# The norms of a two-layer diffusion trunk: where the squares are summed, where the root is read, and who splits the result

## The chip, the cores and the metric

The kernel runs on one core of a Trainium2 chip. The metric is the device time of one launch in microseconds (us). The engines are TensorE (PE; its weight loads are PEld), VectorE (DVE), ScalarE (ACT), GpSimd (POOL) and SyncE (SP), which issues the transfers. Each engine works through its own queue in order; SBUF is the on-chip memory, PSUM the banks that PE writes its products to.

## The reference, cut to what matters

A latent stream x of 512 tokens and a context of 256 tokens, 1024 features each, go through two layers. Every layer has a token-mixing sub-layer (attention, gated DeltaNet and gated linear attention that share one input projection and one output projection) and a convolutional feed-forward (FFN). Around both stands the same sandwich of norms:

```python
def rmsnorm(x, g):
    xf = x.astype(F32)
    y = xf * lax.rsqrt(jnp.mean(xf * xf, axis=-1, keepdims=True) + NORM_EPS)
    return y.astype(x.dtype) * g

def modulate(h, shift, scale):
    return h * (1 + scale) + shift
```

A sub-layer computes x + gate * rmsnorm(sub(modulate(rmsnorm(x, g_pre), shift, scale)), g_post); shift, scale and gate come from a product of the conditioning vector with w_ada. The mean of squares goes over the 1024 features of a token.

## The kernel before, in words

Activations lie feature-major: eight tiles (k = 0 to 7) of 128 features, each with all 768 tokens (the context in columns 0 to 255, named CS, the latents in 256 to 767, named XS). A norm over the features is therefore a sum over the eight tiles and over the 128 partitions of each. There are sixteen such norms: eight prenorms (three of 512 tokens, five of 256; the two at the very start are computed ahead of their scaling) and eight posts (two of 512, six of 256). The first layer works on 512 latents and then on 256 context tokens; the second layer's output projection and last FFN part work on two halves of 256 latents, since the context is no longer needed.

`rms` (L492) does this: ACT squares the eight tiles (L505), the even ones and the odd ones are added into two accumulators, the even ones by DVE, the odd ones by POOL (L507). PE multiplies each 128 tokens of both accumulators with a column of ones (tile `ones`), which gives a sum for each token on its partition; ACT takes the root, DVE the reciprocal (`rsqrt`, L243 and L244). A second set of PE products spreads the reciprocal over all partitions, into a second bank of PSUM, and ACT copies it to SBUF as `rb` (L523).

`post` (L526) scales the sub-layer's output with gate and rb (DVE, L533, tile `y`) and adds it to x (L534), even tiles on DVE, odd ones on POOL. `prenorm` (L536) makes the modulated input in two float32r parts, `hh` and `hl`. Even tiles: DVE makes v (L545), ACT adds the shift and rounds to hh (L546), DVE subtracts for hl (L547). Odd tiles: DVE makes v (L549), ACT makes hh (L550) and the unrounded value (L551), POOL subtracts (L552).

All large products are three float32r passes (high times low, low times high, high times high; tile `bb`), L212 by way of the helper `mm`. Their weights arrive as `wr` and are split too: ACT rounds (`wh`, L191), DVE subtracts (`wl`, L192). So DVE's queue holds the norms' steps and the weights' low parts that PE needs next. At the start `ada` (L467) multiplies the conditioning vector with sixteen loads of w_ada (tile `aw`, eight products of two loads each, then a small product of `part`); all eight must be done before the first prenorm can scale. Single banks of PSUM are handed out in turn (`ab`, tags a to d).

The order on every engine is set by a scheduler that lays the whole program out beforehand with its own estimates; the order in which the code issues the steps and the number of buffers of each tag steer it, so that a change in the norms moves instructions elsewhere too.

Of the kernel before, what the change touches and what calls it, by code (L numbers as in the profile page):

```python
# [11 lines left out]
F32 = mybir.dt.float32  # L12
# [8 lines left out]
KT = 8  # L21
# [11 lines left out]
# columns of the feature-major parameter array  # L33
# [3 lines left out]
PA = (0, 2, 4, 6)  # L37
WP = ()
SQB = 3
# [15 lines left out]
SQ0, MG, PR = 0, 0, 0  # L55
ACB, RBB = 4, 2
WB, RB = 3, 2
R3, B3 = 0, 0
NF = 3                  # tiles of the GDN preparation under way at a time
# columns of the constant array  # L60
# [50 lines left out]
def rope_tables():  # L111
    """cos and signed sin on the rope rows, ones on the others: even heads, odd heads"""
# [23 lines left out]
class Net:  # L136
# [46 lines left out]
    def ab(self, tags=None):  # L183
        """a bank of PSUM, out of those of the phase or of the chain of work named"""
        tags = tags or self.tags
        self.turn[tags] = n = self.turn.get(tags, -1) + 1
        t = tags[n % len(tags)]
        return self.ps.tile([128, 512], F32, name=self.nm(t), tag=t, bufs=1)
# [8 lines left out]
    def wsplit(self, src, n=1024):  # L197
        """loads [128, n] weights and splits them in two float32r parts, 512 columns a piece"""
# [18 lines left out]
    def fprod(self, ps, wh, wl, xh, xl, segs, nk, order=None, off=256):  # L217
        """ps[:, 256 + token] = sum over k of w[:, k]^T x[k], in three float32r passes"""
# [13 lines left out]
    def pace(self, n):  # L232
        """some steps of the products that fill the tensor engine beside chains of small ones"""
# [7 lines left out]
    def rsqrt(self, out, ss, scale, bias):  # L241
        """out = 1 / sqrt(scale * ss + bias), small tiles"""
# [18 lines left out]
    def main(self):  # L261
# [20 lines left out]
        # the first two modulations lead; the norm needs all of x, then them  # L282
# [28 lines left out]
    def layer(self, l, later):  # L311
# [9 lines left out]
        # token mixing  # L321
# [22 lines left out]
        # pairs that need nothing of what the scan holds up run beside its end  # L344
# [28 lines left out]
        # output projection, norm, residual  # L373
# [17 lines left out]
        # feed-forward  # L391
# [10 lines left out]
        def tail(s):  # L402
            """norm, residual, and the next layer's first norm for a segment"""
# [33 lines left out]
    def coefs(self, s, r):  # L437
        """modulation of sub-layer s for latent (0) or context (1) tokens: scale [128, 8], shift [128, 8]"""
# [8 lines left out]
    def gate(self, s):  # L447
        """gate times post-norm gain of sub-layer s: [128, 8] for latent and context tokens"""
# [17 lines left out]
    def ada(self, l, mods, raw=None):  # L466
        """products of the conditioning vectors with w_ada, a load at a time"""  # L467
# [24 lines left out]
    def rms(self, N, src, a, b, copy=False):  # L492
# [1057 lines left out]
```

## Time and profile before

| | |
|---|---|
| time, median of 3 runs | 2308.41 us (2298.91 to 2311.32) |
| span of the profiled execution | 2300.4 us |
| PE busy | 2073.8 us, 90% of the span |
| PEld busy | 1695.2 us, 74% |
| DVE busy | 1308.2 us, 57% |
| ACT busy | 1008.7 us, 44% |
| POOL busy | 536.1 us, 23% |

The profile is of one execution. Busy shares are averages: in the long product stretches PE is busy all the time, at the scans and at the norms it is not. Rows of a stretch are read together with what ended the idle time before them.

### The profile page before, as it was taken

To read this page: it belongs to the slowest core of one execution; us is meant where nothing else is said; L and a number is where in the kernel's file an instruction comes from. 1 tells how busy PE (TensorE), PEld (TensorE's weight loads), DVE (VectorE), ACT (ScalarE), POOL (GpSimd) and SP (SyncE) were. 2 spreads that over 40 slices of the span, in tenths; PEclk is the share of its full clock that TensorE was granted. 3 is DMA by queue.
4 is the path that set the end of the run, shared out by engine and by line. 5 is a ranking of instruction groups with operands and counts; after the bars stand their busy time and mean duration, and the time that the engine had idled before them with its cause. 6 is when DMAs were issued, how large, how long until landed. Compare 5 with 4: busy or idle time off the path is not lost. (4 is left out here: it accounts for less than half of the span.)

```text
span 2300.4 us, 44608 instructions
## 1 busy us (share of the span) xinstructions
PE 2073.8 (90%) x18168; PEld 1695.2 (74%) x18168; DVE 1308.2 (57%) x2474; ACT 1008.7 (44%) x1927; POOL 536.1 (23%) x897
## 2 busy tenths in 40 slices
PE   6898999988988799999999889899978887999996
PEld 3676877766667578888888677777766666888886
DVE  3454435678736743445454774555657647655566
ACT  4653323566454533323232456434446346543333
POOL 1442122245402310101010334322123503211102
PEclk9899999999899899999999987999988888999997
DMA  7233344421042454421222332122402043332322
GB/s 259 73 111 104 102 152 151 148 79 58 8 158 92 142 169 165 163 85 56 65 66 72 111 98 76 42 73 93 149 26 95 6 166 95 111 98 95 101 92 92
DMA packets 121998, 235.64 MB, mean 102 GB/s; under 512 B 9088, under 2 KB 74048, under 8 KB 121792
## 3 DMA queue, kind: packets, MB, share of 16 engines
q1 hardware_dynamic: 121792, 232.78, 30.9%
q8 instruction: 143, 2.34, 0.4%
q14 instruction: 63, 0.52, 0.1%
HBM read 204.04 MB, written 28.70 MB: 101 GB/s over the span
## 5 line engine op out<-in xcount | busy, mean ns | idle before, releaser
L212 PE MATMUL bb<-hh,wl 128*128 128x512 f32 (+1 forms) x1520 | 549.3, 362 | 17.6 <-DVE wl L192 8.0
L212 PE MATMUL bb<-hl,wh 128*128 128x512 f32 (+1 forms) x1520 | 545.0, 359 | 7.3 <-POOL hl L552 5.5
L192 DVE TENSOR_TENSOR wl<-wr,wh 128x512 fp32r<-128x512 f32 (+2 forms) x452 | 336.2, 747 | 364.8 <-ACT wh L191 363.7
L212 PE MATMUL bb<-hh,wh 128*128 128x512 f32 (+1 forms) x1520 | 541.2, 356 | 0.0
L191 ACT CAST wh<-wr 128x512 fp32r<-128x512 f32 (+2 forms) x452 | 274.4, 612 | 527.4 <-PE bb L212 359.2
L212 PEld LDWEIGHTS bb<-hh,wl 128*128 128x128 f32 x1520 | 294.2, 194 | 74.2 <-issue 11.1
L212 PEld LDWEIGHTS bb<-hl,wh 128*128 128x128 f32 x1520 | 294.2, 194 | 53.0 <-POOL hl L552 9.8
L212 PEld LDWEIGHTS bb<-hh,wh 128*128 128x128 f32 x1520 | 294.4, 194 | 39.9 <-issue 2.4
L212 PE MATMUL bb<-g,wh 128*128 128x512 f32 (+1 forms) x1024 | 264.0, 349 | 2.3 <-DVE g L192 2.3
L1426 POOL TENSOR_SCALAR y<-u,fmt 128x512 f32<-128x512 f32 (+2 forms) x88 | 81.3, 925 | 524.1 <-ACT u L811 522.6
L212 PEld LDWEIGHTS bb<-g,wh 128*128 128x128 f32 x1024 | 181.9, 195 | 27.6 <-DVE g L192 3.3
L212 PE MATMUL bb<-g,wl 128*128 128x512 f32 (+1 forms) x512 | 180.6, 354 | 21.5 <-DVE wl L192 8.5
L212 PEld LDWEIGHTS bb<-g,wl 128*128 128x128 f32 x512 | 99.4, 195 | 36.9 <-ACT g L191 9.3
L212 PE MATMUL bb<-mh,wl 128*128 128x256 f32 (+1 forms) x256 | 84.8, 332 | 22.5 <-DVE wl L192 15.4
L811 ACT ACTIVATE u<-bb,fmt 128x512 f32<-128x512 f32 (+1 forms) x118 | 69.1, 614 | 81.1 <-PE bb L212 81.0
L1453 DVE TENSOR_TENSOR y<-y,bb 128x512 f32<-128x512 f32 (+2 forms) x80 | 54.7, 685 | 82.9 <-PE bb L212 82.8
L507 POOL TENSOR_TENSOR acc<-acc,sq 128x256 f32<-128x256 f32 (+1 forms) x48 | 49.4, 1031 | 185.2 <-ACT sq L505 184.5
L1427 DVE SCALAR_TENSOR_TENSOR y<-u,fmt,y 128x512 f32<-128x512 f32 (+2 forms) x88 | 72.3, 822 | 28.9 <-POOL y L1426 28.9
L1365 ACT ACTIVATE P<-bb,ast,srq 128x768 f32<-128x768 f32 (+1 forms) x80 | 72.5, 907 | 30.5 <-DVE ast L1363 20.2
L212 PE MATMUL bb<-ml,wh 128*128 128x256 f32 (+1 forms) x256 | 83.5, 326 | 0.5
L212 PE MATMUL bb<-mh,wh 128*128 128x256 f32 (+1 forms) x256 | 82.2, 321 | 0.0
L1362 DVE TENSOR_REDUCE ast<-bb 128x1 f32<-128x768 f32 (+1 forms) x80 | 67.3, 844 | 25.3 <-PE bb L212 25.0
(509 smaller groups left out, 3720.1 us busy)
## 6 DMA issues: line engine op xcount, KB each, us to landing
wr<-in_ffn_w_in SPq DMA_DIRECT2D x92, 512.0 KB, 3.5
wr<-in_w_ada SPq DMA_DIRECT2D x80, 512.0 KB, 4.4
wr<-in_ffn_w_out SPq DMA_DIRECT2D x48, 512.0 KB, 3.5
wr<-in_w_in SPq DMA_DIRECT2D x40, 512.0 KB, 4.0
wr<-in_w_out SPq DMA_DIRECT2D x32, 512.0 KB, 3.5
aw<-in_w_ada SPq DMA_DIRECT2D x16, 512.0 KB, 8.9
x<-in_xT SPq DMA_DIRECT2D x16, 384.0 KB, 8.5
wr<-in_w_uq SPq DMA_DIRECT2D x16, 192.0 KB, 2.6
```

The source lines that it names most:

```text
L191: self.nc.scalar.copy(hi, src)
L192: (eng or self.nc.vector).tensor_tensor(lo, src, hi.bitcast(F32), op=ALU.subtract)
L212: self.nc.tensor.matmul(out, l, r, start=start, stop=stop)
L507: (nc.vector, nc.gpsimd)[k % 2].tensor_tensor(acc[k % 2], acc[k % 2], sq, op=ALU.add)
L811: nc.scalar.activation(u[:, a + o:b + o], ps[:, off + a:off + b], AF.Identity, bias=bias)
L1362: nc.vector.reduce_max(st[:, 0:1], sc, axis=AX)
L1365: nc.scalar.activation(P[:, :w], sc, AF.Exp, bias=st[:, 0:1], scale=self.srq[:, t:t + 1], accum_out=st[:, 1:2])
L1426: nc.gpsimd.tensor_scalar(yv, u[:, lo + 1:lo + 1 + n], cw[1], self.fm(P_FCB + i), op0=ALU.mult, op1=ALU.add)
L1427: nc.vector.scalar_tensor_tensor(yv, u[:, lo:lo + n], cw[0], yv, op0=ALU.mult, op1=ALU.add)
L1453: nc.vector.tensor_tensor(y, y, p, op=ALU.add)
```

## The change

Four things change, in `rms`, `post` and `prenorm`, with two constants. For a prenorm (`pe=True`, and for the two norms at the start) the adds of the squares go: PE multiplies each of the eight tiles of squares with the column of ones and lets PSUM add them up. For a post (`pe=False`) one accumulator takes all eight, added by DVE alone. Sums and the spread reciprocal root share one bank of PSUM, and DVE reads the root from there; only the two norms at the start copy it to SBUF (`copy=True`). In `prenorm` all eight tiles take the path of the even ones, so POOL does no part of a split. Five tiles hold squares or v where three did (SQB). The constants SQ0, MG, PR and PA, which were zero or chose the even tiles, go with their branches. Comments are left out; line numbers move by two to seven.

```diff
-SQB = 3
+SQB = 5
...
-ACB, RBB = 4, 2
+ACB, RBB = 2, 2
...
-    def rms(self, N, src, a, b, copy=False):
+    def rms(self, N, src, a, b, copy=False, pe=True):
...
-        acc = [tile("acc", ACB) for _ in range(2)]
-        for k in range(KT):
-            sq = acc[k] if k < 2 else tile("sq", SQB)
-            nc.scalar.activation(sq, src[k][:, a:b], AF.Square)
-            if k >= 2:
-                (nc.vector, nc.gpsimd)[k % 2].tensor_tensor(acc[k % 2], acc[k % 2], sq, op=ALU.add)
...
         ps = self.ab()
-        for t in range(nt):
-            for i, z in enumerate(acc):
-                self.mm(ps[:, t:t + 1], z[:, t * 128:(t + 1) * 128], self.ones[:, 0:1], i == 0, i == len(acc) - 1)
+        if pe:
+            for k in range(KT):
+                sq = tile("sq", SQB)
+                nc.scalar.activation(sq, src[k][:, a:b], AF.Square)
+                for t in range(nt):
+                    self.mm(ps[:, t:t + 1], sq[:, t * 128:(t + 1) * 128], self.ones[:, 0:1], k + t == 0, k == KT - 1 and t == nt - 1)
+        else:
+            acc = tile("acc", ACB)
+            for k in range(KT):
+                sq = tile("sq", SQB) if k else acc
+                nc.scalar.activation(sq, src[k][:, a:b], AF.Square)
+                if k:
+                    nc.vector.tensor_tensor(acc, acc, sq, op=ALU.add)
+            for t in range(nt):
+                self.mm(ps[:, t:t + 1], acc[:, t * 128:(t + 1) * 128], self.ones[:, 0:1], True, True)
         r = self.small(4, "rms", 4)[:, :nt]
         self.rsqrt(r, ps[:, :nt], 1.0 / D, self.eps[:, 0:1])
-        ps = self.ab()
         for t in range(nt):
             self.mm(ps[:, t * 128:(t + 1) * 128], r[:, t:t + 1].to_broadcast([128, 128]), self.c("ident"), True, True)
-        if PR and not copy:
+        if not copy:
             return ps[:, :n]
...
-        rb = self.rms(N, y, a, b)
+        rb = self.rms(N, y, a, b, pe=False)
...
-            if k in PA:
-                nc.vector.scalar_tensor_tensor(v, self.xt[k][:, a:b], sc[:, k:k + 1], rb, op0=ALU.mult, op1=ALU.mult)
-                nc.scalar.activation(hi, v, AF.Identity, bias=sh[:, k:k + 1])
-                nc.vector.scalar_tensor_tensor(lo, v, sh[:, k:k + 1], hi.bitcast(F32), op0=ALU.add, op1=ALU.subtract)
-            else:
-                nc.vector.tensor_tensor(v, self.xt[k][:, a:b], rb, op=ALU.mult)
-                nc.scalar.activation(hi, v, AF.Identity, bias=sh[:, k:k + 1], scale=sc[:, k:k + 1])
-                nc.scalar.activation(v, v, AF.Identity, bias=sh[:, k:k + 1], scale=sc[:, k:k + 1])
-                nc.gpsimd.tensor_tensor(lo, v, hi.bitcast(F32), op=ALU.subtract)
+            nc.vector.scalar_tensor_tensor(v, self.xt[k][:, a:b], sc[:, k:k + 1], rb, op0=ALU.mult, op1=ALU.mult)
+            nc.scalar.activation(hi, v, AF.Identity, bias=sh[:, k:k + 1])
+            nc.vector.scalar_tensor_tensor(lo, v, sh[:, k:k + 1], hi.bitcast(F32), op0=ALU.add, op1=ALU.subtract)
```

The order that the scheduler makes of it is shown at three places. The first is PE's queue at the start of the program, where the modulation products (out of `aw` and `cTs`, with a small one out of `part`) and the sums of squares (out of `ones`) stand. Before:

```order
L212 MATMUL c_146<-aw_142,cTs 32x256 x4
L212 MATMUL c_146<-aw_144,cTs 32x256 x4
L212 MATMUL c_146<-cst,part_155 128x2 x2
L212 MATMUL d_168<-aw_164,cTs 32x256 x4
L212 MATMUL d_168<-aw_166,cTs 32x256 x4
L212 MATMUL d_168<-cst,part_177 128x2 x2
L212 MATMUL a_190<-aw_186,cTs 32x256 x4
L212 MATMUL a_190<-aw_188,cTs 32x256 x4
L212 MATMUL a_190<-cst,part_199 128x2 x2
L212 MATMUL b_236<-ones,acc_214 128x1
L212 MATMUL b_236<-ones,acc_215 128x1
```

After, from the same place:

```order
L210 MATMUL b_214<-ones,sq_215 128x1 x4
L210 MATMUL b_214<-ones,sq_221 128x1 x4
L210 MATMUL c_146<-aw_142,cTs 32x256 x4
L210 MATMUL c_146<-aw_144,cTs 32x256 x4
L210 MATMUL b_214<-ones,sq_227 128x1 x4
L210 MATMUL b_214<-ones,sq_233 128x1 x4
L210 MATMUL d_168<-aw_164,cTs 32x256 x3
L210 MATMUL c_146<-cst,part_155 128x2 x2
L210 MATMUL d_168<-aw_164,cTs 32x256
L210 MATMUL d_168<-aw_166,cTs 32x256 x4
L210 MATMUL b_214<-ones,sq_239 128x1 x4
L210 MATMUL b_214<-ones,sq_245 128x1 x2
```

The sums moved from behind the fifth modulation product to between the second and all that follow, and there are four for each tile of squares of the latents where two accumulators had eight in all; the last three modulation products stand behind the context's sums too.

The second place is PE's queue in the first layer's output projection, where the context's first two products (`bb`) run while the latents' post is under way. Before, the post's sums:

```order
L212 MATMUL bb_8084<-mh_6338,wh_8080 128x256
L212 MATMUL bb_8084<-mh_6331,wl_8077 128x256
L212 MATMUL c_7921<-ones,acc_7900 128x1
L212 MATMUL c_7921<-ones,acc_7899 128x1
L212 MATMUL c_7921<-ones,acc_7900 128x1
L212 MATMUL c_7921<-ones,acc_7899 128x1
L212 MATMUL c_7921<-ones,acc_7900 128x1
L212 MATMUL c_7921<-ones,acc_7899 128x1
L212 MATMUL c_7921<-ones,acc_7900 128x1
L212 MATMUL bb_8084<-ml_6339,wh_8076 128x256
```

After:

```order
L210 MATMUL bb_8067<-mh_6348,wl_8060 128x256
L210 MATMUL bb_8067<-ml_6356,wh_8059 128x256
L210 MATMUL bb_8067<-mh_6348,wh_8059 128x256
L210 MATMUL a_7913<-ones,acc_7914 128x1 x4
L210 MATMUL bb_8103<-mh_6349,wl_8100 128x256
```

The sums moved from the middle of the context's second product to right behind its first, and there are four where there were eight.

The third place is PE's queue at the second layer's last prenorm, ahead of the FFN's products. Before:

```order
L212 MATMUL d_20363<-hh_19383,wh_20370 128x256
L212 MATMUL a_20199<-ones,acc_20177 128x1
L212 MATMUL a_20199<-ones,acc_20178 128x1
L212 MATMUL a_20199<-ones,acc_20177 128x1
L212 MATMUL a_20199<-ones,acc_20178 128x1
L212 MATMUL b_20207<-cst,rms_20204 128x128 x2
L212 MATMUL bb_20258<-hh_19376,wl_20401 128x256
```

After:

```order
L210 MATMUL d_20367<-hh_19397,wh_20374 128x256
L210 MATMUL b_20182<-ones,sq_20183 128x1 x2
L210 MATMUL b_20182<-ones,sq_20187 128x1 x2
L210 MATMUL b_20182<-ones,sq_20191 128x1 x2
L210 MATMUL b_20182<-ones,sq_20195 128x1 x2
L210 MATMUL b_20182<-ones,sq_20199 128x1 x2
L210 MATMUL b_20182<-ones,sq_20203 128x1 x2
L210 MATMUL b_20182<-ones,sq_20207 128x1 x2
L210 MATMUL b_20182<-ones,sq_20211 128x1 x2
L210 MATMUL b_20182<-cst,rms_20215 128x128 x2
L210 MATMUL bb_20262<-hh_19390,wl_20405 128x256
```

Nothing moved past the sums here; four became sixteen, with the same work ahead of them and behind.

## Rows read from the trace of the kernel before

**Rows 1.** The page's first part: busy us (share of the span) and instructions.

```profile
PE 2073.8 (90%) x18168; PEld 1695.2 (74%) x18168; DVE 1308.2 (57%) x2474; ACT 1008.7 (44%) x1927; POOL 536.1 (23%) x897
```

**Rows 2.** Windows: length, busy us of PE, PEld, DVE, ACT, POOL, clock, DMA.

```profile
0.00:80.00 80.00, 52.96 (x262) 31.90 (x262) 29.70 (x60) 37.01 (x68) 15.38 (x18) 0.87 0.60 203
700.00:822.00 122.00, 94.35 (x634) 77.39 (x632) 80.88 (x124) 65.64 (x127) 38.84 (x52) 0.89 0.42 138
1280.00:1400.00 120.00, 98.37 (x495) 82.57 (x494) 89.67 (x139) 66.50 (x121) 44.68 (x48) 0.83 0.33 106
1850.00:1965.00 115.00, 88.02 (x634) 82.84 (x633) 74.54 (x135) 65.79 (x145) 28.48 (x38) 0.85 0.43 138
2250.00:2300.00 50.00, 30.19 (x208) 28.83 (x207) 33.91 (x66) 17.43 (x37) 12.44 (x15) 0.74 0.28 91
```

**Rows 3.** A window, and PE's timeline (start, length, what, [idle before]), program's start.

```profile
12.00:46.00 34.00, 26.04 (x169) 16.28 (x168) 7.91 (x21) 15.74 (x33) 6.10 (x6) 1.00 0.98 339
...
30.66 3.15 PE L212 MATMUL b<-ones,acc 128*128 128x1 f32 x14 [0.81 <-POOL acc L507]
...
35.45 1.93 PE L212 MATMUL b<-aw,cTs 128*32 128x256 f32 x16
...
43.34 1.33 PE L212 MATMUL d<-aw,cTs 128*32 128x256 f32 x16
```

**Rows 4.** DVE's and POOL's timeline during the first split of x.

```profile
46.59 0.75 DVE L545 SCALAR_TENSOR_TENSOR v<-x,msc,rb 128x512 f32<-128x512 f32 x1
47.26 0.69 DVE L549 TENSOR_TENSOR v<-x,rb 128x512 f32<-128x512 f32 x1
...
50.69 1.65 DVE L545 SCALAR_TENSOR_TENSOR v<-x,msc,rb 128x512 f32<-128x512 f32 x1
...
57.62 0.47 DVE L545 SCALAR_TENSOR_TENSOR v<-x,msc,rb 128x256 f32<-128x256 f32 x1
58.01 0.41 DVE L549 TENSOR_TENSOR v<-x,rb 128x256 f32<-128x256 f32 x1
...
66.61 0.72 POOL L552 TENSOR_TENSOR hl<-v,hh 128x256 fp32r<-128x256 f32 x1 [1.57 <-ACT v L551]
```

**Rows 5.** DVE's groups of the whole span by line and shape: count | busy, mean ns.

```profile
L533 DVE SCALAR_TENSOR_TENSOR y<-y,mg,rb 128x256 f32<-128x256 f32 x48 | 28.0, 651 | 1.8 <-ACT rb L523 1.8
L192 DVE TENSOR_TENSOR g<-y,g 128x512 fp32r<-128x512 f32 x40 | 27.8, 696 | 18.0 <-ACT g L191 18.0
...
L1453 DVE TENSOR_TENSOR y<-y,bb 128x512 f32<-128x512 f32 x32 | 21.9, 687 | 29.8 <-PE bb L212 29.8
...
L533 DVE SCALAR_TENSOR_TENSOR y<-y,mg,rb 128x512 f32<-128x512 f32 x16 | 15.0, 1005 | 0.9 <-ACT rb L523 0.9
```

**Rows 6.** Timeline of PE and DVE in the first layer's output projection.

```profile
710.30 1.62 PE L212 MATMUL c<-ones,acc 128*128 128x1 f32 x14
...
716.40 8.44 DVE L533 SCALAR_TENSOR_TENSOR y<-y,mg,rb 128x512 f32<-128x512 f32 x8 [0.28 <-ACT rb L523]
...
728.37 0.58 PE L212 MATMUL bb<-mh,wl 128*128 128x256 f32 x1 [8.50 <-DVE wl L192]
```

**Rows 7.** PE's timeline at the end of the first layer's FFN.

```profile
1318.92 0.58 PE L212 MATMUL bb<-g,wl 128*128 128x256 f32 x1 [8.51 <-DVE wl L192]
```

**Rows 8.** PE's timeline at the second layer's last prenorm.

```profile
1944.03 2.02 PE L212 MATMUL a<-ones,acc 128*128 128x1 f32 x8 [8.68 <-DVE acc L507]
```

**Rows 9.** Timeline of all engines at the end of the program.

```profile
2285.79 0.72 POOL L507 TENSOR_TENSOR acc<-acc,sq 128x256 f32<-128x256 f32 x1 [2.63 <-ACT sq L505]
2286.56 1.44 PE L212 MATMUL c<-ones,acc 128*128 128x1 f32 x6 [1.67 <-POOL acc L507]
...
2289.87 0.37 ACT L523 COPY rb<-d 128x256 f32<-128x256 f32 x1 [1.57 <-PE d L212]
2290.28 4.65 DVE L533 SCALAR_TENSOR_TENSOR y<-y,mg,rb 128x256 f32<-128x256 f32 x8 [1.78 <-ACT rb L523]
```

**Rows 10.** PE's timeline in the last scan of the second layer.

```profile
1853.46 0.44 PE L215 MATMUL d<-cst,s 128*128 128x128 f32 x2 [2.80 <-POOL s L1061]
```

More of the change, by code (lines that the diff above doesn't have):

```diff
@@ L36 @@
 P_PO, P_N = P_N, P_N + 16
-PA = (0, 2, 4, 6)
 WP = ()
-SQB = 3
+SQB = 5
 PD = 3
@@ L54 @@
 NL = 2
-SQ0, MG, PR = 0, 0, 0
-ACB, RBB = 4, 2
+ACB, RBB = 2, 2
 WB, RB = 3, 2
@@ L498, in tile @@
             return N.tile([128, 512], F32, name=self.nm(tag), tag=tag, bufs=bufs)[:, :n]
-        if SQ0:
-            nc.scalar.activation(self.small(1, "sq0"), self.eps[:, 0:1], AF.Sqrt)
-        acc = [tile("acc", ACB) for _ in range(2)]
-        for k in range(KT):
-            sq = acc[k] if k < 2 else tile("sq", SQB)
-            nc.scalar.activation(sq, src[k][:, a:b], AF.Square)
-            if k >= 2:
-                (nc.vector, nc.gpsimd)[k % 2].tensor_tensor(acc[k % 2], acc[k % 2], sq, op=ALU.add)
-        if MG:
-            nc.vector.tensor_tensor(acc[0], acc[0], acc[1], op=ALU.add)
-            acc = acc[:1]
-        ps = self.ab()
-        for t in range(nt):
-            for i, z in enumerate(acc):
-                self.mm(ps[:, t:t + 1], z[:, t * 128:(t + 1) * 128], self.ones[:, 0:1], i == 0, i == len(acc) - 1)
+        ps = self.ab()
+        if pe:
[13 more added lines that the diff above has]
+                self.mm(ps[:, t:t + 1], acc[:, t * 128:(t + 1) * 128], self.ones[:, 0:1], True, True)
         r = self.small(4, "rms", 4)[:, :nt]
         self.rsqrt(r, ps[:, :nt], 1.0 / D, self.eps[:, 0:1])
-        ps = self.ab()
         for t in range(nt):
             self.mm(ps[:, t * 128:(t + 1) * 128], r[:, t:t + 1].to_broadcast([128, 128]), self.c("ident"), True, True)
-        if PR and not copy:
+        if not copy:
             return ps[:, :n]
```

## The prediction

> **What bounds the kernel now.** I read the page's busy line first: TensorE (PE) is busy for 2073.8 of 2300.4 us, VectorE (DVE) for 1308.2, GpSimd (POOL) for 536.1 [rows 1]. So a microsecond taken off DVE or POOL is worth something only where PE stands idle, and a microsecond put on PE costs time wherever it does not. The table by stage [rows 2] says where that is: the norms of the two layers lie in five stretches of 80, 122, 120, 115 and 50 us, and there PE is idle for 27, 28, 22, 27 and 20 us, some 123 of its 227 idle microseconds. All sixteen norms lie in them. Then I read the timeline of each stretch for what ends PE's idle time there: at the start it is the first split of x [rows 4], in the projections it is weights' low parts queued on DVE behind a norm's steps [rows 6, 7], in the last norm of a layer and of the kernel it is the norm's own chain [rows 8, 9]. I work on the span of the profiled execution, 2300.4 us. The median of the three runs, 2308.41, is 8 us above it; I take the change of the span over to the median.
>
> **What the change does to PE.** Eight prenorms (three of 512 tokens, five of 256) sum their squares over the features by 8 products per 128 tokens where there were 2: 3 x (32 - 8) + 5 x (16 - 4) = 132 more. The eight posts use 1 where there were 2: 2 x (4 - 8) + 6 x (2 - 4) = 20 fewer. Each such product is two matmul records. Fourteen records took 3.15 us early on and 1.62 us at 710 us [rows 3, 6], so one product costs 0.45 us at the half rate and 0.23 at the full one: 112 more are 26 us of PE at the full rate, 50 at the half. That is the price; the rest is what of it lies in idle time.
>
> **What it does to DVE, ACT and POOL.** POOL loses 80 operations (48 adds of squares, 32 low parts). DVE loses the prenorms' 24 adds, gains 4 adds in each of 8 posts and 32 low parts; ACT loses four passes per prenorm and 14 copies of the reciprocal root. What this is worth is in the stretch that DVE's steps show beside POOL: the post's scaling of 512 tokens averages 1005 ns and of 256 tokens 651 [rows 5], where the same form takes 750 and 470 alone [rows 4]; the prenorm's v at 50.69 took 1.65 us while POOL was at a low part [rows 4]. Now the reciprocal root is read from PSUM. DVE's other step that reads one operand from PSUM, y<-y,bb, averages 687 ns for 512 elements, no more than the same operation with both operands in SBUF, 696 [rows 5]. So I charge nothing for the read and save up to 16 x 0.25 + 48 x 0.18 = 13 us of DVE in the posts, if such a step escapes POOL's.
> [...] No row here shows such a step right beside one of POOL's, so it stands as the ground of the faster rival below.
>
> **Stage by stage.**
> Start (0 to 80 us). Before, PE goes through the eight modulation products as their weights land, and sums the squares from 30.66 in one go. Now 36 more products stand among the modulation products in PE's queue, and the last modulation product, which gates the first v, stands behind all of them. At the half rate of that time they are 36 x 0.45 = 16.3 us. Between 12 and 46 us PE was idle for 34.0 - 26.0 = 8.0 us [rows 3], of which all could take sums. If the rate rises where it did (sixteen modulation records took 1.93 us at 35.45 and 1.33 at 43.34 [rows 3]), 16.3 - 6.9 = 9.4 us are left over at about 41.6, cost 4.7 at the full rate, and 1.1 of idle time is still there: v starts 3.6 us later. If the sums keep PE at the half rate, it is 16.3 - 8.0 plus the 3.6 us of PE work after 41.6 once more, 11.9 us. Against that the split gets shorter: from v at 46.59 to POOL's last low part at 67.33 it took 20.7 us; DVE alone, at a pitch of 0.67 for 512 (46.59 to 47.26) and 0.39 for 256 (57.62 to 58.01) [rows 4], needs 16 x 0.67 + 16 x 0.39 plus two weights' parts of 0.69, 18.3. Sum: +1.2 to +9.5; I take +5, the middle.
> First layer's output projection (700 to 822). The post's sums move ahead of the second small product, the copy of the root goes, so its scaling starts some 3.5 us before 716.40; its eight steps of 8.44 us and the x adds come sooner too, and with them the weights' parts behind them, for which PE waited 8.50 us to 728.37 [rows 6]. But PE has a product fewer to do before that wait, so I count 3 to 6 us gained of the 8.5. Behind it lie 30 more sums, 7 us at the full rate and 13.5 at the half, in a stretch where PE has some 19 us of other idle time; I let half of the 7 go on the path, against about as much won by the unhindered split of the small prenorm. -3 (-9 to +6).
> First layer's feed-forward end (1280 to 1400). The same shape: an 8.51 us wait for a weight's part [rows 7], 30 more sums, POOL out of the way. Less is won, since products there wait for g and its weights in turn. -1 (-5 to +5).
> Second layer's output projection (1850 to 1965). Two rounds of 256 tokens, 24 more sums less 4. In the last one PE has nothing else: four sums took 2.02 us at 1944.03, at the half rate, after POOL's and DVE's adds; sixteen take 7.2 and can start only with the first square, some 3 us before that. v moves by 7.2 - 2.0 - 3.0, less the copy that goes (0.5): +1.7 [rows 8]. The first round puts 10 more sums on PE, 2.3 us, of which I let half stand on the path. +3 (-1 to +6).
> End (2250 to 2300). This chain is the end itself: POOL's last add 0.72 becomes DVE's, some 0.3 shorter; three sums after it at 1.44 become two, 0.96; the copy of 0.37 goes; the eight scalings, 4.65, lose 0.9 at 0.47 each [rows 4, 9]. -2 (-2.5 to +1, since the posts add four DVE operations).
> The rest. The norms take one bank of PSUM in turn where they took two, and the root's bank stays taken until the last step that reads it; so banks and order shift in the scans too. No row prices that; the nearest is a wait of PE in a scan, 2.80 us [rows 10], so I take 0 with two such waits either way (-5 to +5).
> Sum: +5 - 3 - 1 + 3 - 2 = +2 us: 2302.4 for the span, 2310 for the median. Taken as independent, the terms' bounds give some 12 us either way.
>
> **Rivals.**
> Slower, one mechanism: the prenorm's sums run at PE's half rate in front of the work that waits for the norm, and nothing covers them. For it: at the start and at 1944 the rows show just that rate; between 29 and 41 us PE was almost continuously at sums and modulation products and stayed slow. Against it: the sums at 710 us ran at full rate. It prices the start at +9.5, the three projections at +6, +5 and +6, and the end at 0: +26, 2335. It decides from the point where over half of the 132 sums run at half rate with PE's next product behind them.
> Faster: POOL's steps were what stretched DVE's (1.65 us where 0.75 is normal [rows 4]), and DVE's queue is what PE waits for. Then the start is +1, the projections -9, -5 and -1, the end -2.5: -16, 2292. For it: the waits at 728 and 1319 are for DVE [rows 6, 7]. Against it: these waits are mostly due to the order of the queue, in which eight scalings still stand ahead of the weight.
>
> **How the numbers follow.** Measurement tells about 0.5%, 11.5 us, from no change. The forecast, terms that nearly cancel, gets 0.42; slower as in the rival or half-way to it 0.36, since PE's added work is certain and its cover is not; faster 0.22. The forecast's own range is 2299 to 2320. The whole range: 2288 to 2338, from the faster rival's time less a little to the slower one's and a little more.
>
> **What would show it.** Right: the first v at 50 to 58 us and the last low part at 69 to 77; y's scaling in the first projection near 713 and its mean near 470 ns for 256 tokens; sixteen sums at 0.45 each before the last prenorm of the second layer; an end 2 us shorter. Wrong: v at 47 us (the sums found cover or the rate rose early), y's steps still stretched, or waits of PE in the scans that are new.

## The result, and the profile after

The changed kernel takes 2327.98 us (median of 4 runs, 2323.87 to 2332.07) where the kernel before takes 2309.84 (median of 4): a ratio of 1.0091, 95% interval 1.0064 to 1.0119. It is slower by 0.9% (18.1 us, 0.8%, by the medians), inside the range and beyond the bound within which "about the same" was forecast. The profiled execution spans 2322.1 us, 21.7 more than before.

The page of after, first part, answers [rows 1]:

```profile
PE 2113.8 (91%) x18392; PEld 1738.9 (75%) x18392; DVE 1281.3 (55%) x2514; ACT 992.5 (43%) x1888; POOL 448.1 (19%) x817
```

PE has 224 records more, which are the 112 products, and is busy 40 us longer; at the full-rate price of 0.23 us a product they would be 26. POOL and DVE are both less busy, as the prediction had it, and the kernel is slower all the same.

Where the time went is read by cutting both traces at the same steps of the program: the first padded tile `u` of the input projection, the first step of the DeltaNet scan (`Sb`), the first tile of the first output projection (`y<-bb` by ACT), the first accumulation of the FFN's output (`y<-y,bb`), the first tile of the second layer's output projection, and the end. First the windows of before (columns as in [rows 2]: length, then busy us of PE, PEld, DVE, ACT and POOL, clock, DMA):

```profile
0.00:92.90 92.90, 65.30 (x322) 42.36 (x323) 33.45 (x66) 48.32 (x86) 24.63 (x30) 0.85 0.54 183
92.90:273.47 180.57, 172.80 (x3144) 137.99 (x3142) 88.88 (x205) 78.45 (x157) 51.48 (x90) 0.99 0.34 109
273.47:669.83 396.36, 355.33 (x3319) 278.92 (x3319) 248.28 (x594) 187.51 (x381) 123.31 (x168) 0.92 0.32 105
669.83:1005.29 335.46, 306.77 (x1976) 253.03 (x1975) 162.10 (x257) 139.39 (x261) 58.53 (x111) 0.96 0.43 140
1005.29:1867.93 862.64, 778.70 (x7352) 642.51 (x7352) 506.74 (x933) 366.42 (x692) 202.22 (x337) 0.92 0.23 76
1867.93:2300.41 432.48, 394.93 (x2064) 340.37 (x2062) 268.73 (x422) 188.60 (x354) 75.92 (x162) 0.95 0.32 104
```

The same six of after:

```profile
0.00:102.16 102.16, 81.11 (x395) 57.93 (x396) 27.86 (x67) 45.46 (x79) 7.75 (x15) 0.90 0.48 163
102.16:303.09 200.93, 181.37 (x3149) 143.85 (x3148) 91.44 (x207) 79.01 (x159) 53.60 (x91) 0.94 0.31 100
303.09:697.10 394.01, 353.78 (x3311) 277.62 (x3311) 248.08 (x593) 186.65 (x379) 122.25 (x168) 0.92 0.33 106
697.10:1034.84 337.74, 318.72 (x2036) 266.15 (x2035) 153.16 (x268) 131.49 (x249) 33.81 (x91) 0.94 0.43 139
1034.84:1893.23 858.39, 775.84 (x7412) 644.45 (x7412) 497.20 (x943) 367.11 (x685) 177.74 (x317) 0.94 0.23 76
1893.23:2322.09 428.86, 403.02 (x2096) 348.89 (x2094) 263.51 (x440) 182.82 (x340) 52.94 (x136) 0.95 0.33 105
```

The differences are +9.3 (start), +20.4 (projection and DeltaNet preparation of the first layer), -2.4 (its scans and attention), +2.3 (its output projection and the FFN's start), -4.3 (the rest of the FFN, the norms at its end, the second layer's mixing) and -3.6 (the second layer's rest). The two last stretches hold ten of the sixteen norms and got shorter; the largest loss is in a stretch that holds none. There PE did the same work (3144 and 3149 records), with 172.80 us busy before and 181.37 after, at a mean clock of 0.99 and 0.94, and stood idle 19.6 us instead of 7.8.

The -4.3 does not belong to norms either. Cut once more at the second layer's first `Sb`, the stretch up to it, with four norms at the FFN's end, takes 560.6 us before and 560.7 after; what got shorter is the second layer's scans and attention behind it, where no norm lies (before, then after):

```profile
1565.89:1867.93 302.04, 251.32 (x2414) 193.65 (x2413) 189.48 (x439) 140.90 (x275) 79.81 (x119) 0.88 0.24 80
1595.56:1893.23 297.67, 246.35 (x2420) 190.60 (x2420) 190.52 (x439) 143.05 (x277) 83.55 (x120) 0.90 0.25 82
```

Likewise the second layer's output projection, up to the first accumulation of its FFN's output, takes 198.1 us before and 198.0 after, so that the -3.6 lies behind it.

The start in after, PE's timeline:

```profile
13.84 3.57 PE L210 MATMUL b<-ones,sq 128*128 128x1 f32 x16 [0.32 <-DVE modT L486]
...
31.67 1.01 PE L210 MATMUL d<-cst,part 128*128 128x2 f32 x4
...
45.11 2.99 PE L210 MATMUL c<-ones,sq 128*128 128x1 f32 x14
...
53.73 0.61 PE L210 MATMUL d<-cst,part 128*128 128x2 f32 x4
...
58.85 0.49 PE L210 MATMUL bb<-hh,wl 128*128 128x512 f32 x1 [2.27 <-ACT hh L544]
```

and DVE's:

```profile
57.29 3.40 DVE L543 SCALAR_TENSOR_TENSOR v<-x,msc,rb 128x512 f32<-128x512 f32 x5
...
74.44 0.49 DVE L545 SCALAR_TENSOR_TENSOR hl<-v,msh,hh 128x256 fp32r<-128x256 f32 x1
```

Sixteen records of sums take 3.57 us, 0.45 a product, the half rate, and nearly so still at 45 us (0.43). The small product of `part`, 1.01 us at 31.67, takes 0.61 at 53.73: the full rate came only between 45 and 53.73. The rates are read from the records' lengths; the clock column says 1.00 for both profiles' first 46 us, [rows 3] included, and does not show them. The first v starts at 57.29 where it started at 46.59 [rows 4]; the split then takes 17.6 us where it took 20.7.

The long wait without a releaser in the preparation, PE's timeline:

```profile
232.90 0.58 PE L210 MATMUL b<-r,s 32*32 32x64 f32 x26 [3.33 <-issue]
...
259.27 0.81 PE L210 MATMUL a<-cst,part 128*128 128x2 f32 x4 [4.24 <-issue]
```

"Issue" is time in which PE waited for nothing that the profile shows. In the same stretch of before the longest such wait is 1.64 us.

The norms' own steps, DVE's groups of after, answer [rows 5]:

```profile
L532 DVE SCALAR_TENSOR_TENSOR y<-y,mg,a 128x512 f32<-128x512 f32 x16 | 10.7, 743 | 0.6 <-PE a L210 0.6
L532 DVE SCALAR_TENSOR_TENSOR y<-y,mg,c 128x256 f32<-128x256 f32 x24 | 9.6, 473 | 0.0
```

The scalings that averaged 1005 and 651 ns take 743 and 473, though POOL still adds x beside them.

The first layer's output projection in after, DVE and PE, answers [rows 6]:

```profile
739.71 5.36 DVE L532 SCALAR_TENSOR_TENSOR y<-y,mg,a 128x512 f32<-128x512 f32 x8 [0.59 <-PE a L210]
...
748.00 0.58 PE L210 MATMUL bb<-mh,wl 128*128 128x256 f32 x1 [5.49 <-DVE wl L190]
752.00 10.55 PE L210 MATMUL b<-ones,sq 128*128 128x1 f32 x64
```

Eight scalings in 5.36 us for 8.44, a wait of 5.49 for 8.50; and then 32 sums of the prenorm in one piece, 10.55 us, with the products queued behind them. The gain and the price stand 4 us apart.

The end of the first layer's FFN, answering [rows 7], has the same shape, with nearly all its sums at the half rate (24 products in 10.23 us):

```profile
1343.76 0.58 PE L210 MATMUL bb<-g,wl 128*128 128x256 f32 x1 [4.68 <-DVE wl L190]
1345.42 3.41 PE L210 MATMUL b<-ones,sq 128*128 128x1 f32 x16
1349.26 10.23 PE L210 MATMUL b<-ones,sq 128*128 128x1 f32 x48
```

The second layer's last prenorm and the end, answering [rows 8] and [rows 9]:

```profile
1967.58 4.19 PE L210 MATMUL b<-ones,sq 128*128 128x1 f32 x32 [1.03 <-ACT sq L503]
...
2310.36 0.42 DVE L512 TENSOR_TENSOR acc<-acc,sq 128x256 f32<-128x256 f32 x1 [0.54 <-ACT sq L510]
2310.93 0.58 PE L210 MATMUL d<-ones,acc 128*128 128x1 f32 x4 [1.57 <-DVE acc L512]
...
2313.11 3.22 DVE L532 SCALAR_TENSOR_TENSOR y<-y,mg,d 128x256 f32<-128x256 f32 x8 [1.10 <-PE d L210]
```

### The profile page after: what moved, and what is told of

Its sections match the earlier page's. It is cut to its first block, busy times and chain, and to the rows that moved or that the text cites. A ratio compares the mean times of both kernels' runs of the same rounds, so it can differ in the third digit from the quotient of the medians.

```text
span 2322.1 us, 44925 instructions
## 1 busy us (share of the span) xinstructions
PE 2113.8 (91%) x18392; PEld 1738.9 (75%) x18392; DVE 1281.3 (55%) x2514; ACT 992.5 (43%) x1888; POOL 448.1 (19%) x817
## 5 line engine op out<-in xcount | busy, mean ns | idle before, releaser
L190 DVE TENSOR_TENSOR wl<-wr,wh 128x512 fp32r<-128x512 f32 (+2 forms) x452 | 330.7, 734 | 375.3 <-ACT wh L189 373.8
L210 PEld LDWEIGHTS bb<-hh,wl 128*128 128x128 f32 x1520 | 294.4, 194 | 67.5 <-issue 11.6
L210 PE MATMUL bb<-g,wl 128*128 128x512 f32 (+1 forms) x512 | 180.3, 353 | 17.6 <-DVE y L1446 7.6
L1420 DVE SCALAR_TENSOR_TENSOR y<-u,fmt,y 128x512 f32<-128x512 f32 (+2 forms) x88 | 72.6, 825 | 31.7 <-POOL y L1419 31.7
L1421 DVE SCALAR_TENSOR_TENSOR y<-u,fmt,y 128x512 f32<-128x512 f32 (+2 forms) x88 | 73.3, 833 | 2.5
```

The lines of the kernel that those rows point to most:

```text
L190: (eng or self.nc.vector).tensor_tensor(lo, src, hi.bitcast(F32), op=ALU.subtract)
L210: self.nc.tensor.matmul(out, l, r, start=start, stop=stop)
L1420: nc.vector.scalar_tensor_tensor(yv, u[:, lo:lo + n], cw[0], yv, op0=ALU.mult, op1=ALU.add)
L1421: nc.vector.scalar_tensor_tensor(yv, u[:, lo + 2:lo + 2 + n], cw[2], yv, op0=ALU.mult, op1=ALU.add)
```

## The experiments

Theory 1 was that the added sums on PE cost time wherever they lie in front of work that waits for the norm, at the start first of all. Theory 2 was that the order of the first layer's preparation, which moves with any change in the norms, decides the largest difference. Against both stood the idea that a faster DVE ought to have paid for it. Twelve kernels took the change apart: ten are the kernel before with one, two or three things done, two are the changed kernel with something undone. The cuts below write each edit as a change of the kernels shown; in the runs themselves tables by kind of norm (`SUMS`, `ROOT`) and a constant (`BANKS`) choose the same branches. Times are medians; each ratio is to the runs of the kernel before that it shared, whose medians were 2306.3 to 2307.0.

| kernel | what differs | us | ratio to before, 95% |
|---|---|---|---|
| b_init_pe | before, start's squares summed on PE | 2330.74 | 1.0084 (1.0054 to 1.0113) |
| b_pre_pe | before, six prenorms' squares summed on PE | 2337.14 | 1.0104 (1.0072 to 1.0136) |
| b_split | before, split by DVE alone | 2306.42 | 0.9992 (0.9961 to 1.0023) |
| b_post_one | before, posts' squares added by DVE alone | 2300.15 | 0.9969 (0.9944 to 0.9994) |
| b_bank1 | before, sums and root share a bank | 2299.18 | 0.9960 (0.9932 to 0.9987) |
| b_root | before, root left in PSUM | 2281.63 | 0.9880 (0.9826 to 0.9934) |
| b_root_in_posts | before, root left in PSUM for posts only | 2281.14 | 0.9880 (0.9849 to 0.9911) |
| b_x_adds_dve | before, x adds by DVE alone | 2294.25 | 0.9943 (0.9923 to 0.9963) |
| a_init_two | after, start's squares as before | 2318.29 | 1.0049 (1.0023 to 1.0075) |
| a_no_pe_sums | after, all of PE's sums undone | 2302.53 | 0.9977 (0.9958 to 0.9995) |
| b_root_post | before, root in PSUM, posts by DVE alone | 2279.03 | 0.9863 (0.9821 to 0.9905) |
| b_root_post_bank1 | the same, one bank | 2273.70 | 0.9844 (0.9812 to 0.9876) |

**The start's sums.** In b_init_pe only the two norms at the start take the path of after:

```diff
-        rbs = [self.rms(N, self.xt, *s, True) for s in (XS, CS)]
+        rbs = [self.rms(N, self.xt, *s, True, pe=True) for s in (XS, CS)]
```

> The kernel before with one thing of the change: the two norms at the start sum their squares on PE (48 products where there were 12), all else as before. Theory 1 (the sums stand at half rate among the modulation products and gate the first v): first v at 55 to 58 us where before has 46.6, and the start's loss of 9 to 10 us stays to the end, about +9 us in all. Theory 2 (the loss between 205 and 303 us belongs to the order of the first layer's projection and DeltaNet preparation, which every change at the start reshuffles): PE's waits marked issue between 200 and 300 us, 3.3 and 4.2 us in after, may appear here too, and then it is +15 to +25. Rival (the half-rate sums are hidden by the shorter split of after and the start is not what costs): +2 us or less.

Its start takes 101.9 us to the first u, +9.0, as in after. What follows is no less dear: the preparation took 192.6 us for 180.6. In all it is 24 us by the medians (12 to 26 by the ratio's interval), more than the 9 of the start. The profiled execution is its slowest, 2344.0 us, so its later stretches are not used.

```profile
0.00:101.87 101.87, 86.90 (x394) 60.67 (x395) 29.25 (x60) 48.91 (x85) 17.51 (x23) 0.92 0.48 164
101.87:294.44 192.57, 179.50 (x3151) 143.35 (x3150) 90.13 (x207) 81.53 (x160) 52.62 (x91) 0.95 0.32 104
```

Theory 1 and the first half of theory 2 both hold: the sums cost what was forecast at the start, and the preparation got longer with no norm in it. But its waits marked issue were 2.2 us at most in that stretch, not 3 and 4, so those two waits are not the whole of what lengthens it. Its first v came at 58.3 us, just behind the 55 to 58 expected.

The opposite edit, the changed kernel with the start as before:

```diff
-        rbs = [self.rms(N, self.xt, *s, True) for s in (XS, CS)]
+        rbs = [self.rms(N, self.xt, *s, True, pe="two") for s in (XS, CS)]
...
-ACB, RBB = 2, 2
+ACB, RBB = 4, 2
```

("two" stands for the two accumulators of before.)

> The changed kernel with the two norms at the start summed as before (two accumulators on DVE and POOL, 12 products on PE), all else as changed. Theory 1: first v back at 46 to 47 us, first product's end at 66 to 67 against 75.5, so 9 to 10 us less than after at that point. Theory 2: if the loss between 205 and 303 us stands or falls with the order of that stretch, the waits marked issue there are under 2 us each, or still there; with them gone it is some 24 to 27 us faster than after (2300 to 2304), with them still there some 9 to 12 us faster (about 2316). Rival (both losses have one cause, the PE sums of the prenorms): no more than 3 us faster than after.

It is 9.7 us faster than after, the smaller of the two amounts. Yet after's two long waits marked issue are gone (the longest in the preparation is 2.84 us), and for that case the expectation was 24 to 27 us: the loss does not hang on those two waits. The profiled execution is its slowest (2328.9 us), 5 us longer than the profiled one of after, so only the places can be read from it. The start is back (95.4 us), the preparation took 188.2 and the scans 406.9, where after had 200.9 and 394.0: what the one gains the other gives back.

```profile
95.41:283.59 188.18, 177.70 (x3105) 144.25 (x3104) 89.27 (x203) 79.36 (x159) 53.19 (x91) 0.96 0.33 107
283.59:690.53 406.94, 355.42 (x3360) 276.25 (x3358) 246.25 (x599) 187.72 (x382) 123.33 (x168) 0.93 0.32 104
```

It also bears on the rate at the start. With the sums of before, its products of `part` and the first of x still ran at the half rate, until 57.6 us:

```profile
47.23 1.01 PE L214 MATMUL b<-cst,part 128*128 128x2 f32 x4 [0.54 <-ACT part L487]
...
57.14 0.63 PE L214 MATMUL bb<-hl,wh 128*128 128x512 f32 x1
...
57.85 0.39 PE L214 MATMUL bb<-hh,wl 128*128 128x512 f32 x1
```

So the many sums at the start go along with a late full rate in after, but are not shown to be its cause.

**The root in PSUM.** Here `rms` returns the bank instead of the copy, for all but the start:

```diff
-        if PR and not copy:
+        if not copy:
             return ps[:, :n]
```

> The kernel before with one thing of the change: 14 of the 16 norms leave the reciprocal root in PSUM and DVE reads it there, no copy by ACT. The order of PE in the first layer up to the output projection is that of before. Theory (a DVE step with one operand in PSUM runs beside POOL undisturbed): the scaling steps of post average 740 and 475 ns, as in after, where before has 1005 and 651; the end gets 1.5 to 2.5 us shorter, PE's wait of 8.5 us at 728 gets 2 to 3 us shorter; in all 4 to 10 us faster than before. Rival (these waits are set by the order of DVE's queue, or the bank held by the root delays others): within 3 us of before.

The sign was right and the size too small: -25 us, against an expected -4 to -10. The scalings take 740 and 475 ns. DVE's and PE's timeline at the places of [rows 6] and [rows 7]:

```profile
716.90 5.35 DVE L548 SCALAR_TENSOR_TENSOR y<-y,mg,d 128x512 f32<-128x512 f32 x8
...
725.78 0.58 PE L214 MATMUL bb<-mh,wl 128*128 128x256 f32 x1 [5.05 <-DVE wl L194]
...
1309.75 0.58 PE L214 MATMUL bb<-g,wl 128*128 128x256 f32 x1 [4.68 <-DVE wl L194]
```

The wait of 8.50 us became 5.05, that of 8.51 at the end of the FFN [rows 7] became 4.68, and the clock fell less around the second: from 1280 to 1400 us PE's mean clock was 0.83 before and is 0.89 here, its busy time 104 us for 98, though the two windows do not hold the same work (this kernel is 5 to 9 us ahead there). So the gain is more than the two waits, and goes along with more time at the full rate behind them. By stretches it is -6 in the first output projection, -10 in the FFN's rest and the second layer's mixing, -6 in what follows.

Which of the 14 roots does it:

```diff
-        rb = self.rms(N, y, a, b)
+        rb = self.rms(N, y, a, b)                   # in post: returns ps[:, :n]
...
         rb = self.rms(N, self.xt, a, b) if rb is None else rb     # in prenorm: as before, copied
```

> The kernel before with the root left in PSUM in the eight posts only; the prenorms keep the copy. If the gain of 25 us is the y steps that escape POOL's x adds, nearly all of it is here: 2281 to 2289. If it is the copy that goes ahead of each norm's first step, a bit over half: 2292 to 2297. If it is the prenorms' v beside POOL's low parts, little: 2300 and more.

All of it is in the eight posts. And to see whether it is POOL that stretched those steps, or the operand's place that makes them short, POOL was taken away with both operands still in SBUF:

```diff
-            (nc.vector, nc.gpsimd)[k % 2].tensor_tensor(xk, xk, yk, op=ALU.add)
+            nc.vector.tensor_tensor(xk, xk, yk, op=ALU.add)
```

> The kernel before with all eight x adds of a post on DVE, none on POOL; the root is copied to SBUF as before. If POOL's x adds are what stretches the y steps, these average 740 and 475 ns here with both operands in SBUF; DVE pays 4 more adds per post (0.41 or 0.68 us), so the first weight after a post comes 0 to 1 us earlier than before and the time is -8 to +4 from before. Rival (the y steps are long because both operands come from SBUF, whatever POOL does): still about 1005 and 650 ns, and +5 to +15 us.

```profile
L548 DVE SCALAR_TENSOR_TENSOR y<-y,mg,rb 128x256 f32<-128x256 f32 x48 | 19.5, 477 | 1.8 <-ACT rb L539 1.8
L548 DVE SCALAR_TENSOR_TENSOR y<-y,mg,rb 128x512 f32<-128x512 f32 x16 | 10.9, 753 | 0.9 <-ACT rb L539 0.9
```

With POOL away, a step with two operands in SBUF took 753 and 477 ns, close to what it took beside POOL with one in SBUF and one in PSUM (740 and 475 in b_root); beside POOL with both in SBUF it took 1005 and 651 (before). So it is POOL's adds beside a step with two operands in SBUF that cost 0.25 and 0.17 us a step, and reading the root from PSUM avoids that without giving the adds up. Even this kernel is 12 us faster than before, more than the 8 that were expected at most.

**The posts' squares by DVE.**

```diff
-        acc = [tile("acc", ACB) for _ in range(2)]
+        acc = tile("acc", ACB)                      # in post: 7 adds by DVE, none by POOL
```

> The kernel before with one thing of the change: the eight posts add their squares with DVE alone into one accumulator (7 adds for 3 on DVE and 3 on POOL; half as many products with ones). PE's order in the first layer up to the output projection is that of before. Theory: the end loses POOL's last add (0.7 against 0.4) and a product, about 1 us; elsewhere the four more adds lie in DVE's idle time; -1 to -3 us in all. Rival (DVE's queue is what PE waits for, so more adds delay the weights' parts): +2 to +6 us.

-6.6 us by the medians, more than the 1 to 3 forecast, though the interval (1 to 13 us) reaches that far; the rival (later weights) is out.

**Root and posts together.**

> The kernel before with the two parts of the change that ran faster alone: 14 norms leave the reciprocal root in PSUM, and the posts add their squares on DVE alone. If both act at different places (the y steps beside POOL; POOL's last add and a product before the root) their gains add: 25 + 6.6, so 2275 to 2281. Rival (both shorten the same chain, or the gain of one was a lucky order of the second layer): 2281 to 2300.

2279.03 us: inside the expectation's range. It is 2.6 us below b_root; with intervals of some 10 us either way that does not tell whether the 6.6 us add in full.

**The split by DVE alone.**

```diff
-PA = (0, 2, 4, 6)
+PA = (0, 1, 2, 3, 4, 5, 6, 7)
```

> The kernel before with one part of the change: all eight tiles of a prenorm are split by DVE (and ACT's one pass), none by POOL. Theory (DVE without POOL beside it is quicker than both with each other): the first split ends 2 to 3 us earlier (65 us against 67.3); the prenorms later 1 to 3 us each; -5 to -10 in all. Rival (the order of the first layer's DeltaNet preparation changes with it, and that decides): first split as said, but between 200 and 300 us a shift of over 5 us either way that has no norm in it.

No difference (0.9992, 0.9961 to 1.0023). The preparation took 185.7 us for 180.6 and the scans 399.7 for 396.4, which is the rival's shift of over 5 us with no norm in it; the later stretches gave most of it back. The first split did end 2.1 us earlier (65.25), as expected, but the first u came no earlier (93.7 us for 92.9), and of the 5 to 10 us forecast the medians show none.

**The prenorms' sums.**

```diff
-        rb = self.rms(N, self.xt, a, b) if rb is None else rb
+        rb = self.rms(N, self.xt, a, b, pe=True) if rb is None else rb
...
-SQB = 3
+SQB = 5
```

> The kernel before with one part of the change: six prenorms (not the two at the start) sum their squares on PE (112 products where there were 28), with five buffers of squares as in after. Theory (the sums cost PE what they take, half of it covered): 84 products more at 0.23 to 0.45 us are 19 to 38 us; +8 to +20 in all, to be seen at 730 to 800, 1340 to 1400 and 1900 to 1965 us. Rival (they stand where PE waits anyway and spare DVE and POOL the adds): within 4 us of before at those three places. What appears between 200 and 660 us is order alone, since no norm of that stretch is changed.

The expectation's count was wrong: six prenorms make 128 products where there were 32, so 96 more, 22 us at the full rate and 43 at the half. Measured +30 us by the medians (the ratio's interval is 17 to 31). The three stretches with norms show it, +9, +7 and +4; the preparation (181.5) and the scans (398.8) are those of before within 3 us. PE's timeline in the first output projection:

```profile
732.28 3.58 PE L214 MATMUL a<-ones,sq 128*128 128x1 f32 x16 [6.36 <-ACT sq L506]
738.21 10.23 PE L214 MATMUL a<-ones,sq 128*128 128x1 f32 x48
```

PE reaches the sums before the squares are there, waits 6.36 us for them, and then does 24 products in 10.23 us, at the half rate (0.43 each), with its next product behind.

**A bank less, no work changed.**

```diff
-        ps = self.ab()
         for t in range(nt):
             self.mm(ps[:, t * 128:(t + 1) * 128], r[:, t:t + 1].to_broadcast([128, 128]), self.c("ident"), True, True)
```

> The kernel before with one part of the change that adds and removes no work: sums and spread root share one bank of PSUM, so the turns of the banks differ and with them the order of PE from the first layer's DeltaNet preparation on. Theory (the order of the preparation and the scans is worth 10 us and more either way): shifts of 5 us or more between 150 and 660 us and between 1400 and 1850, where no norm lies. Rival (such shifts need the change at the start): within 3 us of before all along.

-7.8 us. The preparation and the scans are as long as before (180.1 and 396.4) although the order inside them is another, so in the first layer the forecast of theory 2 fails: not every reshuffle costs or gives 10 us there. In the second layer it holds: the scans and attention behind its first `Sb`, where no norm lies, took 294.4 us for 302.0, which is the whole gain; the first output projection gave 3.7 us (331.8 for 335.5), and the start and the FFN took 3.5 back.

**The changed kernel without PE's sums.** Both kinds of sums undone, with four buffers of `acc` as in a_init_two, all else as changed:

```diff
-        rbs = [self.rms(N, self.xt, *s, True) for s in (XS, CS)]
+        rbs = [self.rms(N, self.xt, *s, True, pe="two") for s in (XS, CS)]
...
-        rb = self.rms(N, self.xt, a, b) if rb is None else rb
+        rb = self.rms(N, self.xt, a, b, pe="two") if rb is None else rb
```

> The changed kernel with every prenorm's and the start's squares summed as before (two accumulators on DVE and POOL); the posts, the root in PSUM, the one bank and DVE's split stay as changed. If the 132 products more on PE are what made the change slower, and the parts add (root -25, posts -7, bank -8, split -1 as measured alone), it is 2262 to 2280, and faster than before. Rival (the loss lies in the order of the first layer's preparation, which is here that of the changed kernel with the old start): 2300 to 2315.

2302.53 us. It is faster than before, by 0.2%, but far from the 2262 to 2280 that the parts add up to; the rival's range holds it. Its windows of the preparation and the scans, and under them those of the three good parts together:

```profile
92.30:283.69 191.39, 180.43 (x3106) 145.99 (x3105) 89.69 (x204) 79.55 (x159) 53.19 (x91) 0.95 0.32 105
283.69:690.09 406.40, 355.35 (x3360) 276.36 (x3358) 246.63 (x599) 187.85 (x382) 124.04 (x168) 0.93 0.31 104
```

```profile
95.39:275.51 180.12, 175.37 (x3157) 142.09 (x3156) 90.31 (x205) 79.13 (x158) 52.24 (x90) 0.97 0.34 110
275.51:673.13 397.62, 357.50 (x3306) 278.15 (x3305) 245.69 (x593) 190.19 (x381) 121.48 (x168) 0.93 0.32 105
```

The first loses 11 and 10 us there against before, and a_init_two, which has the same order of PE in those two stretches, loses 8 and 11: two kernels, two executions, the same place. The second, with the order of b_bank1, loses nothing. The products there are the same in all of them. Taken over all traces, the length of the two stretches together goes with the order of PE's records: six kernels that share one order (before, b_root, b_root_in_posts, b_post_one, b_root_post and b_x_adds_dve) take 576.9 to 580.5 us there, the two with b_bank1's order 576.5 and 577.7, the two with this one 595.1 and 597.8. After has an order of its own and takes 594.9. So an order of the first layer's preparation and scans can cost 20 us; those of the changed kernel do, in after in the preparation, in these two in both.

Two things set a_no_pe_sums apart from the kernel of the three good parts, b_root_post_bank1: the split by DVE alone and the five tiles of squares. Together they go with 29 us of the medians, 20 in these two stretches and 8 in the first output projection (334.2 for 325.9). The split alone cost nothing (b_split); the five tiles alone were not run, nor either one on top of the three good parts.

**The best of the parts.** Root in PSUM, posts by DVE alone, one bank; the sums and the split stay as they were before:

> The kernel before with the root left in PSUM, the posts' squares added on DVE alone, and one bank for sums and root; the split stays between DVE and POOL. If the bank's 8 us add to the 28 of the other two: 2270 to 2274. Rival (the 8 us alone were one order of many): 2275 to 2290.

2273.70 us (2270.23 to 2275.97), 0.9844 of before (0.9812 to 0.9876): it beats both kernels, by 33 and 54 us. The gain of one bank adds to the other two, as far as the intervals tell.

## Why the prediction came out as it did

- **PE's added sums.** The price was right (0.45 us a product at the start, from [rows 3]), the cover too generous. At the start I took +5 between +1.2 and +9.5; the first u came 9.3 us later, at the upper bound. The failing step is the rise of the rate at 41.6: at 45 us the sums still ran at 0.43. So the value taken should have been the upper end, not the middle. In the prenorms I let about half of 7 us stand on the path in the first output projection; taken alone they cost 9 us there and 30 us in all. Undone in the changed kernel they are worth 25 us: 9.7 at the start, 15.8 in the prenorms, the latter between two kernels of the same order in the first layer's preparation and scans.
- **The root in PSUM.** The mechanism was seen (13 us of DVE saved, as the ground of the faster rival) and then priced at a few microseconds, because the order of the queue was thought to hold the waits up. Alone it is worth 25 us. The failing step is the sentence that these waits "are mostly due to the order of the queue": 3.5 and 3.8 of 8.5 us went at two such waits, more than a third, and the clock fell less around the second.
- **The split.** 17.6 us measured for the first one, 18.3 forecast.
- **Output projection of the first layer.** -3 forecast, +2.3 measured. The gain came as priced, at its lower end (the wait got 3.0 us shorter, of 3 to 6). The sums were under-priced: 32 of them took 10.55 us, where the 30 added were priced at 7 and half of that was taken.
- **End of the first layer's FFN.** -1 forecast, +0.1 measured: the wait got 3.8 us shorter, and the 32 sums behind it ran at the half rate, 13.6 us in two pieces.
- **Second layer's output projection and last prenorm.** +3 forecast, -0.1 measured (198.0 us for 198.1). In the last prenorm the sixteen sums took 4.19 us and not 7.2: they ran near the full rate (0.26 each), after a wait of 1.03 us where PE had waited 8.68 before.
- **The end.** -2 forecast with a bound of -2.5; from the last y on it is 15.7 us before and 12.7 after, -3.0. The scalings gave 1.4, more than the 0.9 taken.
- **The rest, "0 (-5 to +5)".** This is the term that failed most: +20.4 in the first layer's preparation, -2.4 in its scans, -4.4 in the second layer's scans, 13.6 in all; the five terms with norms in them sum to +8.1 where +2 was forecast. None of the sixteen norms lies there. Two such waits were allowed for, one of 2.80 us each; the trace has waits of 3.33 and 4.24 us, and PE's busy time for the same work rose by 8.6 us with the lower clock. New waits of PE in the scans were named as a sign of being wrong; they came, in the preparation ahead of the scans.

Put in a row, the medians account for the result: before 2306.3; with the root in PSUM, the posts by DVE and one bank 2273.7; with the split by DVE and five tiles 2302.5; with the prenorms' sums on PE 2318.3; with the start's too (and two buffers of `acc`), which is after, 2328.0. So the change gains 33 us, gives 29 back at the split and the tiles, which go along with the slower order, and loses 25 on PE's sums. (In the runs of the result before took 2309.8, so there it is 18.)

The range held; the forecast of about no change, which had the largest chance (0.42), did not. The slower rival (0.36) had the sums' price right: over half of the prenorms' sums ran at the half rate (some 215 of 352 records in the trace of after), and undone they are worth 25 us against its +26. That its total also came near +18 is luck: it left out the 33 us gained and the 29 given back, and these nearly cancel.

What stays open: why PE waits in the preparation where the profile shows nothing to wait for, and why its order of small matmuls is worth 20 us in one arrangement and nothing in another. The kernels show where and how much, not the cause; no run kept after's order with the start of before.

## What to carry to other kernels

The reduction that was moved from idle engines to the busiest one cost a good part of its own time there (25 us, of 26 to 50 us of products), and more where its products ran at the half rate (0.43 to 0.45 us a product, against 0.23 at the full one): price such a move at the rate that the rows of that place show. The DVE steps beside GpSimd's adds took 743 and 473 ns with one operand left in PSUM, where a product had put it anyway (after), and 1005 and 651 with both in SBUF (before); that was worth 25 us (b_root), more than every rearrangement of who adds what, so it is a place to try first. And with a scheduler that lays out the whole program, take a change apart and keep the parts that stand alone, since an edit at one place can cost 20 us in a stretch that it does not touch.

## What the runs showed of the hardware that was not expected

- A scaling step with two operands in SBUF took 1005 ns (512 columns) beside GpSimd's adds (before), 753 without them (b_x_adds_dve), and 743 beside them with one operand in PSUM (after). PSUM as a source cost nothing here (these 743 ns against the 753). Before copied the root out of PSUM ahead of the eight steps of a norm that read it; leaving that copy out of 14 norms gained 25 us (b_root), all of it in the posts, whose steps stand beside GpSimd's adds (b_root_in_posts).
- At the start of after PE ran at the half rate from 14 us (0.45 us a sum) to 45 us (0.43) and beyond, although it was busy nearly all that time; the product of `part` at 53.73 ran at the full one. In before that product was at the full rate by 42.80 us (0.61), in a_init_two, with the same few sums as before, not at 47.23 (1.01).
- Where a wait of PE went from 8.51 us (before) to 4.68 (b_root), the stretch around it (1280 to 1400 us) ran at a mean clock of 0.89 and not 0.83, and the time from the FFN's first accumulation to the second layer's output projection fell by 10 us, more than the wait.
